# Gated outputs in both partition halves, a reordered opening, and a new list of attention steps, in a two-layer encoder step

## The chip, the core and the metric

One core of a Trainium2 chip runs the whole program in one launch. The metric is the device time of one execution in microseconds (us), lower is better. The core has a matrix engine (TensorE, PE in the rows; its weight loads are PEld), three engines for elementwise work (VectorE or DVE, ScalarE or ACT, GpSimd or POOL), a queue engine that issues transfers (SyncE or SP), the on-chip memory SBUF with 128 partitions, and PSUM, 128 partitions too, into which TensorE writes its products.

## What is computed

One step of a streaming encoder of two layers on 512 prompt tokens and 64 sample tokens (576 in all, width 1024, float32). Each layer:

```python
h = rmsnorm(x, g_mix_norm)
qa, ka, va, qg, kg, vg, ag, rg, cq, ckv, kr = split(h @ w_in)
o_a = rmsnorm(stick_breaking_attention(qa, ka, va))        # 4 heads x 64
o_b = rmsnorm(gla(qg, kg, vg, ag), g_gla_out) * silu(rg)   # gated linear attention, 4 heads, 32 -> 64
o_c = rmsnorm(mla(cq, ckv, kr))                            # latent attention, 8 heads x 64
x = x + concat([o_a, o_b, o_c]) @ w_out
x = x + cross_attention(rmsnorm(x), memory)                # 256 memory tokens
x = x + swiglu(rmsnorm(x))                                 # inner width 2816
```

Gated linear attention runs over blocks of 16 tokens. For a block with decayed queries `qt`, keys `kt`, and the state `S` (32 x 64 per head) that all earlier blocks left:

```python
att = where(tril, qt @ kt.T, 0)
o   = qt @ S + att @ v
S   = exp(b_last) * S + kd.T @ v
```

## The kernel before

All activations lie transposed, features on partitions and the 576 tokens along the row. The tokens are cut in two ways: five tiles (`TILES`: four of 128 tokens and one of 64), and two halves of `HF` = 288. Big products are made in about float32 from three products of rounded parts (`mm3`: high by high, high by low, low by high); the parts of an operand, H and L, are made by a copy on ScalarE and a subtraction on VectorE (`split_w`, `XNorm.split`). Small products are plain float32; each such call shows as two passes, two weight loads and two matmuls, in the trace.

**The opening.** SyncE loads three token tiles (`xin`), the first 256 columns of the input projection (`w_first`, buffer `wraw`, 1 MB), and the other two token tiles. TensorE turns each tile with eight transposes; the two evictions of a tile go to ScalarE and VectorE; ScalarE also sums the squares of each tile's rows (`x_squares`). `split_w` cuts the weights into two parts of 128 columns, each rounded and subtracted, and the first half of the tokens is split between these parts (`xn0.split`). Then `x_rstd` brings the norm factors of the rows to all partitions: a diagonal matrix for each tile on VectorE, multiplied by a matrix of equal numbers on TensorE. During the opening the order of ScalarE, VectorE and GpSimd is fixed as it is written (`nc.chain`), that of TensorE is not. The first products follow in `win`, four groups of 24 matmuls: half 0 of the tokens with two groups of 128 columns, then half 1.

**The list of steps.** Within a layer's mixers the units of work are generators that are advanced one step at a time; `STEPS` is a list, written out and used for both layers, of which unit goes next. A capital letter is a task (W the input projection and later output projections' steps, G gains, S and Z old keys, T short turns), a small letter a line of units with its number: a prepares the gated stage, l makes its block states, m scans them (VectorE), n writes its outputs (two steps each: scores, then products), o is the output norm; b is stick-breaking; later letters follow. One step of W is a group of 24 matmuls or a token tile of a projection.

**The gated stage.** `states` makes the sums of each block, `scans` turns them into the states, kept in `U` as 64 x 33 numbers per partition, so that the state of one block is read with a stride of 33 elements (the sample's with a stride of 5). `out` makes the scores of a tile for all four heads, masks them on VectorE (a predicated copy), and then accumulates in one PSUM buffer `po` (tag T, three buffers):

```python
for h in range(4):
    mm(po[0:64, h, 0:rn], vg[0:rn, t, h * 64:h * 64 + 64], at[0:rn, h, 0:rn], h == 0, False)
for n in range(nb):
    mm(po[0:64, :, 16 * n:16 * n + 16], S, qtx[:, :, r0 + 16 * n:r0 + 16 * n + 16], False, n == nb - 1)
```

Four copies, by turns on ScalarE and VectorE, move two heads to partitions 0 to 63 of `G` and two to 64 to 127. Stick-breaking's `tile_attention` already writes the outputs of two heads into the two halves of a PSUM buffer, head by head in turn.

## Time and profile before

| what | value |
|---|---|
| time, median of 3 runs | 1663.23 us (1661.26 to 1664.08) |
| the profiled execution, its own time | 1666.25 us |
| its span, first to last instruction | 1664.5 us |
| mean granted clock of TensorE | 0.994 |
| busy share: TensorE, VectorE, ScalarE, GpSimd | 98%, 73%, 54%, 9% |

The profile is of one execution. A row of the timeline gives start, length, engine, line, operation, output and inputs by their names in the program (`gla0` is the gated stage of layer 0, `sb1` stick-breaking of layer 1), shapes, a count where like rows were merged, and in brackets how long the engine had stood before it and on whose work. Nearly everything passes through one recording helper, so all rows have line 209; they are told apart by names. Matmul ends are modelled and overlap, so the distance between starts is the better price. The granted clock is given as a share of full speed: 1.00 is 2.4 GHz and 0.50 is 1.2 GHz.

### The profile page before, as it was taken

The numbers are of one execution on the slowest core, as the hardware profiler recorded it, in microseconds if no ns is written. First come the engines' busy times: TensorE is split into PE (matmuls) and PEld (weight loads), VectorE is DVE, ScalarE is ACT, GpSimd is POOL, SyncE is SP. The second block draws the span as 40 slices with busy tenths as digits, with TensorE's granted clock in tenths as the row PEclk, the third lists the DMA queues.
The fourth block names the chain that finished last, engine by engine and source line by source line (L and its number), as shares of the span: only waits on it lengthen the run. The fifth ranks groups of instructions, "written<-read, shape, count | busy, mean of one in ns | idle before, by whom it ended". The sixth has DMA issues, their size and how long they took to land.

```text
span 1664.5 us, 30858 instructions
## 1 busy us (share of the span) xinstructions
PE 1638.2 (98%) x12279; PEld 1532.3 (92%) x12279; DVE 1216.0 (73%) x2508; ACT 897.1 (54%) x1915; POOL 142.2 (9%) x257
## 2 busy tenths in 40 slices
PE   8999999999999999999999999999999999999998
PEld 7989788699999999999998889877999999999998
DVE  5747798876798767666667488987678877667663
ACT  6436778665754443344443457886667453344431
POOL 3112351000000000000010133300000000000000
PEclk9999999999999999999999999999999999999999
DMA  5322230022123232322223313201211232332321
GB/s 168 118 69 65 75 111 26 27 77 77 52 77 102 77 102 77 102 93 85 81 75 97 93 40 118 67 27 39 89 52 56 97 102 77 102 99 79 101 77 58
DMA packets 113647, 133.30 MB, mean 80 GB/s; under 512 B 10610, under 2 KB 95712, under 8 KB 113504
## 3 DMA queue, kind: packets, MB, share of 16 engines
q1 hardware_dynamic: 113120, 131.30, 25.0%
q8 instruction: 97, 1.59, 0.4%
q14 instruction: 46, 0.38, 0.1%
q0 software_dynamic: 352, 0.03, 0.0%
q10 hardware_dynamic: 32, 0.01, 0.0%
HBM read 123.64 MB, written 7.68 MB: 79 GB/s over the span
## 4 chain that ended last, share of the span: by engine, by line
PE 81%; DVE 7%; issue 4%; ACT 3%; DMA 2%; POOL 1%; ACTq 0%; POOLq 0%; DVEq 0%
PE ffn0.D L209 10%; PE ffn1.D L209 9%; PE ffn0.T L209 7%; PE ffn0.S L209 7%; PE ffn1.T L209 6%; PE ffn1.S L209 6%; PE win1.D L209 6%; PE win0.D L209 4%; PE wout1.D L209 3%; PE wout0.D L209 3%; PE cross1.D L209 2%; PE cross0.D L209 2%; PE cross0.T L209 1%; PE cross1.T L209 1%; PE mlap0.T L209 1%
## 5 line engine op out<-in xcount | busy, mean ns | idle before, releaser
L209 ACT ACTIVATE ffn1.wH<-ffn1.wraw 128x1024 fp32r<-128x1024 f32 x64 | 59.4, 927 | 116.9 <-PE ffn1.T L209 61.7
L209 ACT ACTIVATE ffn0.wH<-ffn0.wraw 128x1024 fp32r<-128x1024 f32 x64 | 59.3, 927 | 111.5 <-PE ffn0.T L209 60.4
L209 DVE TENSOR_TENSOR ffn1.sL<-ffn1.sum,ffn1.sH 128x1024 fp32r<-128x1024 f32 x40 | 48.9, 1222 | 40.0 <-ACT ffn1.sH L209 39.9
L209 DVE TENSOR_TENSOR ffn0.sL<-ffn0.sum,ffn0.sH 128x1024 fp32r<-128x1024 f32 x40 | 48.9, 1222 | 39.6 <-ACT ffn0.sH L209 39.5
L209 DVE TENSOR_TENSOR ffn1.wL<-ffn1.wraw,ffn1.wH 128x1024 fp32r<-128x1024 f32 x64 | 67.6, 1056 | 8.3 <-ACT ffn1.wH L209 7.6
L209 DVE TENSOR_TENSOR ffn0.wL<-ffn0.wraw,ffn0.wH 128x1024 fp32r<-128x1024 f32 x64 | 67.5, 1055 | 8.3 <-ACT ffn0.wH L209 7.6
L209 PE MATMUL ffn0.D<-ffn0.bT,ffn0.sH 128*128 128x288 f32 x320 | 65.3, 296 | 0.1
L209 PE MATMUL ffn1.D<-ffn1.bT,ffn1.sH 128*128 128x288 f32 x320 | 65.1, 295 | 0.1
L209 ACT ACTIVATE ffn1.sH<-ffn1.sum 128x1024 fp32r<-128x1024 f32 x40 | 42.2, 1055 | 21.4 <-PE ffn1.S L209 21.2
L209 ACT ACTIVATE ffn0.sH<-ffn0.sum 128x1024 fp32r<-128x1024 f32 x40 | 42.2, 1055 | 21.1 <-PE ffn0.S L209 21.0
L209 POOL TENSOR_TENSOR win1.s<-win1.vg,rS 128x32 f32<-128x32 f32 (+1 forms) x5 | 2.9, 590 | 581.3 <-DVE win1.vg L209 580.2
L209 PEld LDWEIGHTS ffn0.D<-ffn0.bT,ffn0.sH 128*128 128x128 f32 x320 | 51.6, 189 | 1.0 <-ACT ffn0.part L209 0.6
L209 PEld LDWEIGHTS ffn1.D<-ffn1.bT,ffn1.sH 128*128 128x128 f32 x320 | 51.6, 189 | 0.7 <-ACT ffn1.part L209 0.6
L209 PE MATMUL ffn1.D<-ffn1.bT,ffn1.sL 128*128 128x288 f32 x160 | 47.5, 297 | 0.0
L209 PE MATMUL ffn0.D<-ffn0.bT,ffn0.sL 128*128 128x288 f32 x160 | 47.5, 297 | 0.0
L209 PE MATMUL win1.D<-win1.wH,ffn0.hH 128*128 128x256 f32 (+1 forms) x160 | 47.2, 295 | 0.0
L209 PE MATMUL win0.D<-win0.wH,in.hH 128*128 128x256 f32 (+1 forms) x160 | 47.1, 295 | 0.0
L209 PE MATMUL win0.D<-win0.wL,in.hH 128*128 128x256 f32 (+1 forms) x160 | 46.1, 288 | 0.3 <-DVE win0.wL L209 0.3
L209 PE MATMUL win1.D<-win1.wL,ffn0.hH 128*128 128x256 f32 (+1 forms) x160 | 46.1, 288 | 0.3 <-DVE win1.wL L209 0.3
L209 PE MATMUL win0.D<-win0.wH,in.hL 128*128 128x256 f32 (+1 forms) x160 | 45.9, 287 | 0.0
L209 PE MATMUL win1.D<-win1.wH,ffn0.hL 128*128 128x256 f32 (+1 forms) x160 | 45.9, 287 | 0.0
L209 ACT ACTIVATE ffn0.part<-ffn0.D 128x288 f32<-128x288 f32 x60 | 24.5, 409 | 38.4 <-PE ffn0.D L209 38.4
(972 smaller groups left out, 6522.2 us busy)
## 6 DMA issues: line engine op xcount, KB each, us to landing
ffn0.wraw<-in_w_gate_dram SPq DMA_DIRECT2D x11, 1024.0 KB, 5.3
ffn0.wraw<-in_w_up_dram SPq DMA_DIRECT2D x11, 1024.0 KB, 5.3
ffn0.wraw<-in_w_down_dram SPq DMA_DIRECT2D x11, 1024.0 KB, 5.1
ffn1.wraw<-in_w_gate_dram SPq DMA_DIRECT2D x11, 1024.0 KB, 5.3
ffn1.wraw<-in_w_up_dram SPq DMA_DIRECT2D x11, 1024.0 KB, 5.4
ffn1.wraw<-in_w_down_dram SPq DMA_DIRECT2D x11, 1024.0 KB, 5.0
win1.wraw<-in_w_in_dram SPq DMA_DIRECT2D x7, 1024.0 KB, 5.4
win0.wraw<-in_w_in_dram SPq DMA_DIRECT2D x6, 1024.0 KB, 5.7
```

The costliest lines, as they stand in the source:

```text
L209: r = fn(*args, **kw)
```

## The change

Three parts. First, in `out`, odd blocks of 16 tokens are accumulated in partitions 64 to 127 of `po` and even ones in 0 to 63: attention by values becomes eight calls of half the columns, the states' calls alternate by block, and the eviction becomes eight copies of half the width. Second, the opening turns tiles 0 to 2, splits the weights (loaded in two halves of 128 columns; both low parts on VectorE), and goes to the first product; tiles 3 and 4 are turned between the first and second product, the squares of tile 2 come after that, and the norm rows of tiles 0 to 2 after the second product. TensorE's order is now fixed too, until the last of the four products. Third, `STEPS` is another order of the same steps.

```diff
@@ -39,14 +39,14 @@
 
 
 STEPS = """
-W0*3 G0 W0*4 T0 W0 T1 W0 T2 W0 T3 a0 W0 T4 a0 W0 a0 W0*3 S0*2 l0 W0 l0 S0 l0*2 l1 W0 l1*3 l2 S0 W0 l2 W0 l2*2 l3 S0 W0
-Z0*2 l3*3 l4 S0 Z0 W0 l4*3 Z0 W0 m0 Z0 T5 T6 W0 Z0 m0 W0 n0 n1 T7 T9 n0 n2 n1 n3 n2 n4 n3 n4 T8 o0 W0 o1 o0 o1 i0 j0
-W0*3 b0 j0 W0*2 b1 b0 j0 W0*3 b0 b2 W0 b1 j0 W0 b1 W0 b3 b2 j0 T10 W0 b2 b4 b3 T11 T12 b3 b5 W0 b4 W0 b4 b6 T13 k0 b5
-k0 b5 b7 Y0 p0 b6 k0 T14 b6 Y1 p1 b7 k0 b7 Y2 c0*2 d0 d1 k0 c1 Y3 k0 d2 c1 k0 d0 d3 d1 d4 d2 d5 k0*2 k1 d3 d6 k1 d4 d7
-k1*2 d5 d8 k1*2 d6 d9 e0 k1 d7 k1*2 d8 k1 e1 e2 k1*2 d9 e1 e3 k1 e2 e4 k1*2 f0 e3 f1 e4 k1*2 k2 f0 f1 e5 k2 f0 f2 f1
-f3 k2 e6 e7 f2 f3 e6 e7 f2 f4 f3 f5 e8 k2 e9 f4 f5 k2 e8 f4 f6 f5 e9 f7 f6 f7 f6 k2 f8 f7 e10 k2 e10 f9 f8*2 f10 f9
-k2*3 f10 f9 f11 f10 f12 g0*2 f11 k2 f12 f11 f13 g1 f12 g1 k2 g2 f13 k2 g2 f13 g3 k2*2 g3 k2*2 h1 h0 k3 h2 h1*2 k3*2
-h0*2 h3 h1 h2 h0*2 h2 k3 h2 h1 h3 h2 h3 k3 h3*2 k3*13
+W0*3 G0 W0*4 T0 W0 T1 W0 T2 W0 T3 a0 W0 T4 a0 W0 a0 W0*3 S0*2 l0 W0 l0 S0 W0 l0*2 l1 W0 l1 W0 l1*2 l2 S0 l2 W0 l2*2 l3
+S0 W0 Z0*3 l3*3 l4 S0 Z0 W0 l4*3 W0 m0 Z0 T5 T6 Z0 m0 W0 n1 n0 T7 n0 n2 n1 n3 n2 T9 n4 n3 n4 T8 o0 W0 o1 o0 W0 o1 i0
+j0 W0*2 b0 j0 W0*2 b1 b0 j0 W0*3 b0 b2 W0 b1 j0 W0 b1 b3 W0*2 b2 j0 T10 b2 b4 b3 T12 b3 b5 W0 b4 W0 b4 b6 b5 k0 T11
+T13 k0 b6 b5 b7 Y0 p0 k0 T14 b6 Y1 p1 b7 k0 b7 Y2 c0*2 d0 d1 k0 c1 Y3 k0 d2 d0 k0 d3 d1 d4 d2 d5 k0*2 k1 c1 d3 d6 k1
+d4 d7 k1*2 d5 d8 k1*2 d6 d9 e0 k1 d7 k1*2 d8 e1 e2 k1*3 d9 e1 e3 k1 e2 e4 k1*2 f0 e3 f1 e4 k1*2 k2 f0 f1 e5 k2 f0 f2
+f1 f3 k2 e6 e7 f2 f3 e6 e7 f2 f4 f3 f5 e8 k2 e9 f4 f5 k2 e8 f4 f6 f5 e9 f7 f6 f7 f6 k2 f8 f7 e10 k2 e10 f9 f8*2 f10 f9
+k2*2 f10 k2 f9 f10 f11 f12 g0*2 k2 f11 f12 f11 f13 k2 g1 f12 g1 g2 f13 k2 g2 k2 f13 g3 k2 g3 k2*2 h1 h0 k3 h2 h1*2
+k3*2 h0*2 h3 h1 h2 h0*2 h2 k3 h2 h1 h3 h2 h3 k3 h3*2 k3*13
 """
 
 
@@ -339,7 +339,11 @@
     w_first = None
     for t, (c0, n) in enumerate(TILES):
         if t == 3:
-            w_first = fetch_w(I["w_in"][0, :, 768:1024], KD, 256)
+            w_first = clock.tile(wp.tile([128, 2048], F32, tag="wraw", name=nm("wraw"), bufs=2), "wraw", 2)
+            w_first = w_first.rearrange("p (k n) -> p k n", n=256)
+            for c in (0, 128):
+                nc.sync.dma_start(w_first[:, :, c:c + 128],
+                                  I["w_in"][0, :, 768 + c:896 + c].rearrange("(k p) n -> p k n", p=128))
         raw = big(name="xin")[:, 0:D]
         nc.sync.dma_start(raw[0:n, :], I["x_prompt"][0, c0:c0 + n, :] if t < 4 else I["x_sample"][0])
         xraw.append(raw)
@@ -347,7 +351,7 @@
 
     ident = cst([128, 128], "ident")
     make_identity(tc.nc, ident)
-    nc.chain.update(act=None, dve=None, pool=None)
+    nc.chain.update(act=None, dve=None, pool=None, pe=None)
     grow = u("kp", "grow")[0:84, 0:128]
     nc.vector.memset(grow, 1.0)
     for r0, g in ((16, "g_cross_norm"), (32, "g_ffn_norm"), (48, "g_mem_norm")):
@@ -429,7 +433,7 @@
             H, L = (clock.tile(wp.tile([128, 1024], F32R, tag=tag, name=nm(tag), bufs=WB[tag]), tag, WB[tag])
                     [:, 0:nk * ncol].rearrange("p (k n) -> p k n", n=ncol) for tag in ("wH", "wL"))
             copyA(H, raw[:, ks, cs])
-            tt(L, raw[:, ks, cs], H, SUB, nc.gpsimd if between and i else None)
+            tt(L, raw[:, ks, cs], H, SUB)
             parts.append((H, L))
             if between and i == 0:
                 between()
@@ -717,23 +721,32 @@
     def x_squares(t, n):
         act(pt4("sq")[0:n, :], xraw[t][0:n, :], AF.Square, scale=D ** -0.5, accum_out=ss[0:n, t:t + 1])
 
-    def x_rstd(t0, t1):
-
-        d = ps_("T")
+    def x_diags(t0, t1):
+
         diags = u("u", "dg")
         for t in range(t0, t1):
             n = TILES[t][1]
-            dg = diags[0:n, (t - t0) * 128:(t - t0) * 128 + n]
-            nc.vector.tensor_scalar(dg, ident[0:n, 0:n], ss[0:n, t:t + 1], None, op0=MUL)
-            mm(d[:, (t - t0) * 128:(t - t0) * 128 + n], ones_x[0:n, :], dg)
+            nc.vector.tensor_scalar(diags[0:n, (t - t0) * 128:(t - t0) * 128 + n], ident[0:n, 0:n], ss[0:n, t:t + 1], None, op0=MUL)
+        return diags
+
+    def x_rows(t0, t1, diags):
+
+        d = ps_("T")
+        for t in range(t0, t1):
+            n = TILES[t][1]
+            c = slice((t - t0) * 128, (t - t0) * 128 + n)
+            mm(d[:, c], ones_x[0:n, :], diags[0:n, c])
         c0, c1 = TILES[t0][0], sum(TILES[t1 - 1])
         copyA(xn0.rows[:, c0:c1], d[:, 0:c1 - c0], scale=float(D))
 
-    for t, (c0, n) in enumerate(TILES):
-        if t < 3:
-            x_squares(t, n)
+    def x_splits(a, k0, k1):
+        for k in range(k0, k1):
+            xn0.split(k, slice(a * HF, (a + 1) * HF))
+
+    def x_turn(t):
+        c0, n = TILES[t]
         for i in range(0, KD, 4):
-            d = ps_("DTS"[(2 * t + i // 4) % 3])
+            d = ps_("DTS"[(2 * t + i // 4) % 3] if t < 3 else "T")
             for j in range(4):
                 tr(d[:, j * 128:j * 128 + n], xraw[t][0:n, (i + j) * 128:(i + j + 1) * 128])
             src = d.rearrange("p (i c) -> p i c", c=128)[:, :, 0:n]
@@ -741,22 +754,50 @@
                 nc.vector.tensor_copy(X[:, i:i + 4, c0:c0 + n], src)
             else:
                 copyA(X[:, i:i + 4, c0:c0 + n], src)
-        def splits(k0, k1):
-            for k in range(k0, k1):
-                xn0.split(k, slice((t // 2 - 1) * HF, t // 2 * HF))
-
-        if t == 2:
-            rstd_small(ss[:, 0:3], 1.0)
-            w_first = split_w(w_first, between=lambda: splits(0, 4))
-            splits(4, KD)
-        if t == 4:
-            x_rstd(0, 3)
-            splits(0, KD)
-    for t in (3, 4):
-        x_squares(t, TILES[t][1])
-    rstd_small(ss[:, 3:5], 1.0)
-    x_rstd(3, 5)
-    nc.chain.clear()
+
+    for t in range(3):
+        x_turn(t)
+        if t < 2:
+            x_squares(t, 128)
+    w_first = split_w(w_first, between=lambda: x_splits(0, 0, KD))
+
+    def first_products(G):
+
+        ds = []
+        for p in range(2):
+            ds.append(ps_("D")[:, 0:HF])
+            for k in range(KD):
+                mm3(ds[p], w_first[0](k, p * 128, p * 128 + 128), w_first[1](k, p * 128, p * 128 + 128),
+                    xn0.h(k)[:, 0:HF], xn0.l(k)[:, 0:HF], k == 0, k == KD - 1)
+            if not p:
+                for t in (3, 4):
+                    x_turn(t)
+                x_squares(2, 128)
+                rstd_small(ss[:, 0:3], 1.0)
+                x_splits(1, 0, 4)
+                dg = x_diags(0, 3)
+                x_splits(1, 4, KD)
+        x_rows(0, 3, dg)
+        for p in range(2):
+            tt(G[:, p, 0:HF], ds[p], xn0.rows[:, 0:HF], MUL)
+        for t in (3, 4):
+            x_squares(t, TILES[t][1])
+        rstd_small(ss[:, 3:5], 1.0)
+        dg = x_diags(3, 5)
+        yield "d"
+        yield "d"
+        for p in range(2):
+            ds[p] = ps_("D")[:, 0:HF]
+            for k in range(KD):
+                mm3(ds[p], w_first[0](k, p * 128, p * 128 + 128), w_first[1](k, p * 128, p * 128 + 128),
+                    xn0.h(k)[:, HF:T], xn0.l(k)[:, HF:T], k == 0, k == KD - 1)
+        x_rows(3, 5, dg)
+        for p in range(2):
+            tt(G[:, p, HF:T], ds[p], xn0.rows[:, HF:T], MUL)
+        yield "d"
+        yield "d"
+        nc.chain.clear()
+
 
     class Order:
 
@@ -1059,6 +1100,10 @@
             st["krn"] = turn["pool"].tile([128, 288], F32, tag="krn", name=nm("krn"), bufs=1).rearrange("p (t c) -> p t c", c=32)
             w = load_w(wi[:, 768:1024], KD, 256) if l else w_first
             for a in range(2):
+                if not l:
+                    if not a:
+                        yield from first_products(G)
+                    continue
                 for p in range(2):
                     yield from ws_steps(w, p * 128, KD, xn.h, xn.l,
                                         lambda a, cs, d: tt(G[:, p, cs], d, xn.R[:, cs], MUL), [a])
@@ -1403,14 +1448,20 @@
                                           ps[0:rn, :, 0:rn])
                 yield "T"
                 po = ps_("T").rearrange("p (h c) -> p h c", c=128)
+
+                at5, po5 = (x[:, :, 0:rn].rearrange("p h (n b c) -> p h n b c", b=2, c=16) for x in (at, po))
                 for h in range(4):
-                    mm(po[0:64, h, 0:rn], vg[0:rn, t, h * 64:h * 64 + 64], at[0:rn, h, 0:rn], h == 0, False)
+                    for b in range(2):
+                        mm(po5[64 * b:64 * b + 64, h, :, b, :], vg[0:rn, t, h * 64:h * 64 + 64], at5[0:rn, h, :, b, :], h == 0, False)
                 for n in range(nb):
                     S = st["U"][:, :, 8 * t + n] if t < 4 else Us[:, :, n]
-                    mm(po[0:64, :, 16 * n:16 * n + 16], S, qtx[:, :, r0 + 16 * n:r0 + 16 * n + 16], False, n == nb - 1)
-                for p in range(2):
-                    copyA(G[0:64, 1 - p, r0:r0 + rn], po[0:64, 2 * p, 0:rn])
-                    nc.vector.tensor_copy(G[64:128, 1 - p, r0:r0 + rn], po[0:64, 2 * p + 1, 0:rn])
+                    b = n % 2
+                    mm(po[64 * b:64 * b + 64, :, 16 * n:16 * n + 16], S, qtx[:, :, r0 + 16 * n:r0 + 16 * n + 16], False, n >= nb - 2)
+                for b in range(2):
+                    for hh, copy in enumerate((copyA, nc.vector.tensor_copy)):
+                        dst = G[64 * hh:64 * hh + 64, 0:2, r0:r0 + rn].rearrange("p a (n b c) -> p a n b c", b=2, c=16)
+                        for p in range(2):
+                            copy(dst[:, 1 - p, :, b, :], po5[64 * b:64 * b + 64, 2 * p + hh, :, b, :])
 
             phase[0] = f"gla{l}"
             od.line([(["vg"], states(t, r0, rn), None) for t, (r0, rn) in enumerate(TILES)], 1, name="states", tag="T")
```

## Rows read from the trace of the kernel before

**Rows 1.** The page, part 1: engine, busy us, share of the span, instructions.

```profile
PE 1638.2 (98%) x12279; PEld 1532.3 (92%) x12279; DVE 1216.0 (73%) x2508; ACT 897.1 (54%) x1915; POOL 142.2 (9%) x257
```

**Rows 2.** Table by stage: stretch, busy us of each engine, granted clock, DMA.

```profile
12.00:13.00 1.00, 0.71 (x6) 0.72 (x7) 1.00 (x2) 1.00 (x3) 0.89 (x1) 0.92 1.38 150
...
19.50:20.00 0.50, 0.50 (x5) 0.50 (x5) 0.41 (x3) 0.00 (x0) 0.00 (x0) 0.83 1.09 338
...
172.00:174.00 2.00, 1.14 (x4) 0.29 (x2) 2.00 (x3) 1.10 (x3) 1.79 (x4) 0.82 0.00 0
```

**Rows 3.** Timeline of the gated stage, layer 0: start us, length, instruction, count.

```profile
105.55 1.09 PE L209 MATMUL gla0.T<-gla0.u,win0.vg 128*64 128x128 f32 x8
...
106.48 1.98 PE L209 MATMUL gla0.T<-gla0.qtx,gla0.U 128*64 128x64 f32 x16
...
108.39 1.12 PE L209 MATMUL gla0.S<-gla0.qtx,win0.G 128*128 128x512 f32 x2
...
108.80 0.28 DVE L209 COPY win0.G<-gla0.T 64x128 f32<-64x128 f32 x1 [2.78 <-ACT win0.G L209]
...
109.44 1.09 PE L209 MATMUL gla0.T<-gla0.u,win0.vg 128*64 128x128 f32 x8
109.62 0.73 DVE L209 COPY_PREDICATED gla0.u<-trilm,gla0.S 128x512 f32<-128x512 uint32 x1 [0.54 <-PE gla0.S L209]
...
119.30 0.68 PE L209 MATMUL gla0.T<-gla0.u,win0.vg 64*64 64x64 f32 x8
...
119.90 1.12 PE L209 MATMUL gla0.T<-gla0.qtx,win0.vg 128*64 128x64 f32 x8
...
120.95 0.44 PE L209 MATMUL win0.T<-ident,win0.sbk 128*128 128x128 f32 x2
...
121.31 0.22 DVE L209 COPY win0.G<-gla0.T 64x64 f32<-64x64 f32 x1 [0.69 <-ACT win0.G L209]
```

**Rows 4.** Waits of TensorE, 920 to 950 us: total us, times, longest.

```profile
PE gla1.T L209 <- ACT gla1.u L209: 0.7, 1, 0.7
```

**Rows 5.** Instructions on gla0.T, weight loads: ns min/median/max, first and last start.

```profile
L209 PEld LDWEIGHTS gla0.T<-gla0.qtx,gla0.U x64: 191/213/216, 106.4 to 119.0; 128*64 128x64 f32 x64
...
L209 PEld LDWEIGHTS gla0.T<-gla0.u,win0.vg x40: 129/137/137, 105.6 to 119.7; 128*64 128x64 f32 x32, 64*64 64x64 f32 x8
```

**Rows 6.** Timeline of TensorE, stick-breaking of layer 1.

```profile
1003.32 1.09 PE L209 MATMUL sb1.T<-sb1.PT,win1.sbv 128*64 128x128 f32 x16
...
1021.70 0.95 PE L209 MATMUL sb1.T<-sb1.PT,win1.sbv 128*64 128x64 f32 x20
```

**Rows 7.** Timeline of the opening.

```profile
5.85 0.60 ACT L209 ACTIVATE X<-in.D 128x512 f32<-128x512 f32 x1
...
8.05 1.05 ACT L209 ACTIVATE in.sq<-in.xin 128x1024 f32<-128x1024 f32 x1
...
10.46 1.06 ACT L209 ACTIVATE in.wH<-in.wraw 128x1024 fp32r<-128x1024 f32 x1 [0.60 <-DMA in.wraw<-in_w_in_dram]
...
11.55 1.29 DVE L209 TENSOR_TENSOR in.wL<-in.wraw,in.wH 128x1024 fp32r<-128x1024 f32 x1 [0.92 <-ACT in.wH L209]
...
12.29 0.66 PE L209 MATMUL in.D<-ident,in.xin 128*128 128x128 f32 x4 [2.46 <-DMA in.xin<-in_x_prompt_dram]
...
13.88 0.50 PEld L209 LDWEIGHTS in.S<-ident,in.xin 64*128 64x128 f32 x4 [0.52 <-issue]
...
14.93 0.61 PE L209 MATMUL win0.D<-in.hH,in.wH 128*128 128x288 f32 x1
...
23.20 1.38 DVE L209 SCALAR_TENSOR_TENSOR in.hL<-X,gT,in.hH 128x288 fp32r<-128x288 f32 x3
...
29.60 0.85 PE L209 MATMUL in.T<-in.dg,ones_x 128*128 128x128 f32 x4 [0.46 <-DVE in.dg L209]
...
32.16 0.29 PE L209 MATMUL win0.D<-in.hH,in.wL 128*128 128x288 f32 x1
```

**Rows 8.** Timeline of VectorE, 78 to 106 us: the last scan.

```profile
96.98 0.81 DVE L209 TENSOR_TENSOR_SCAN win0.vg<-win0.vg 128x320 f32<-128x320 f32 x1
```

## The prediction

> **What bounds the kernel now.** The page's busy shares come first: TensorE is busy for 98% of the span [rows 1]. So a change pays by taking time out of TensorE's own stream, or by closing one of its few gaps. The next view is the table by stage, with the granted clock: TensorE idles for 2.46 us in the opening, until 12.29; its clock then falls to half and comes back at about 19.7 us; it falls again near 173 us, in the thin part of the stick-breaking stage [rows 2, 7]. A mean clock of 0.994 over 1664.5 us loses 10 us, so about 20 us run at half speed: three stretches of some 6.8 us, the third at the same place of layer 1. The change touches the first and shifts the others. The third view is the timeline of the stage that writes the gated outputs [rows 3], where TensorE runs without a gap in layer 0; the wait list of layer 1 shows one wait of 0.7 us behind it, on the squares of the output norm [rows 4].
>
> **Part 1, the gated outputs.** For one tile of 128 tokens TensorE runs 8 passes of attention by values (four heads, two passes a call; 105.55 to 106.48, 0.93 us, 0.116 a pass), 16 passes of state by query (106.48 to 108.39, 1.91 us, 0.119 a pass), and the scores of a later tile (108.39 to 109.44, 1.05 us) [rows 3]. All outputs lie in partitions 0 to 63. A pass of the states has only 64 columns and costs as much as one of 128: its weights, read with a stride of 33 elements, load in 213 ns, where packed values of the same size take 137 [rows 5]. After the change blocks alternate between the two halves: attention becomes 16 passes of 64 columns, the states stay 16 passes, each on the other half from its neighbour.
>
> What an alternating pass costs stands in stick-breaking's own products, whose heads alternate between the halves. There 16 passes of 128 columns last 1.09 us, just what 8 of them last on one half; less a tail of 0.16 (1.09 against 0.93 above) that is 0.058 a pass against 0.116. And 20 passes of 64 columns last 0.95, less a tail of 0.08 (the last tile's 0.68 against 0.60 to the next start) 0.044 a pass, against 0.075 for that last tile, which has 64 columns on one half (8 passes from 119.30 to 119.90) [rows 3, 6]. The ratios are 0.50 and 0.59. For the states I take the worse: 0.119 becomes 0.070.
>
> One tile: attention 0.93 becomes 16 x 0.044 = 0.70, saving 0.23; states 1.91 become 1.12, saving 0.79; together 1.02, four times a layer, 4.1 us. The last tile, of 64 tokens: attention 0.60 becomes 0.70, losing 0.10; its 8 passes of states, 1.05 (119.90 to 120.95), become 0.62, saving 0.43 [rows 3]. A layer: 4.4 us, **both layers 8.8 us**. No row alternates halves with strided weights, so the bounds: at least the states save nothing, which leaves 4 x 0.23 - 0.10 = 0.82 a layer, 1.6 in all; at most they come down to the 0.044 of packed weights, which saves 1.21 + 0.23 a tile and 0.60 on the last, 6.4 a layer, 12.7 in all. A loss in the passes is excluded by the alternating rows, unless alternation fails altogether (attention then at 0.075 a pass).
>
> The evictions grow from four copies a tile to eight, in pairs by engine. Today VectorE's copy waits for ScalarE's, so the four are one chain, with a masked copy of 0.73 on VectorE in it; a copy of half the width takes 0.22 instead of 0.28 [rows 3]. Eight of these, three changes of engine at 0.04 and the masked copy make 2.6 us a tile. TensorE's period per tile goes from 3.89 to 0.70 + 1.12 + 1.05 = 2.87. The chain fits below that, with three buffers in PSUM between, so I cost it at nothing; if the cover went, every 0.1 us of chain above 2.87 would cost some 0.9 us over both layers' 4.5 tiles.
>
> A rule of the Trainium skill speaks against this part: TensorE: Matmul & The Clock Gate, Part 3, "The mechanism", says that a weight load overlaps with matmuls in flight only where the row group differs, and both halves here share their rows. By it the states' loads would stay as they are, the sum at the lower bound; the stick-breaking rows contradict it for packed weights, and no row decides it for strided ones.
>
> **Part 2, the opening.** Removed from the front: the squares of tile 2, and the transposes of tiles 3 and 4 before the first products. TensorE resumes at 12.29, when tile 3's transfer lands behind the weights; the first product is at 14.93, the last at 32.16 [rows 7]. In the new order ScalarE alternates evictions (0.60) and squares (1.05, and 0.2 for the read of the sum): from the first eviction at 5.85 its steps end at 6.45, 7.70, 8.30, 9.55, 10.15. Then the weights' high part (1.06) ends at 11.2, VectorE's low part (1.29) at 12.5, the activations' first low part (1.38 / 3 = 0.46) at 12.95 [rows 7]. The weights come in two halves; the whole was there at 10.46, so the first half is not late at 10.15 as long as packets of half the size don't slow it. The first product can go at about 11.7, the second waits to 12.95: useful work resumes some 0.45 us after today's 12.29. Gone are 0.52 us of idle between tiles 3 and 4, and 0.46 before the last norm rows (at 29.60) [rows 7]. What comes: in TensorE's new fixed order the norm rows stand between the first two products and the second two, and wait for a chain that begins only when tiles 3 and 4 are evicted: squares of tile 2 on ScalarE, four splits and the diagonals on VectorE. Squares 1.25, the first split on both engines 0.9, three more of 0.46 and a first diagonal of about 0.2 are 3.8 us; 24 products at 0.13 (a row's 0.29 overlaps the next; 0.44 at half clock) cover 3.1 of it. I put 0.7 us of wait there, with the second half's products queued behind it.
>
> The clock: today it fell after the idle 2.46 us and came back 4.8 us after products began (14.93 to 19.7) [rows 2, 7]. If products begin at 12.95 and it follows as it did, it is back at 17.75, 2 us sooner, and half speed costs half: 1.0 us gained. Bounds: nothing, or all 3.4 us if it doesn't fall. The opening: -0.45 + 0.52 + 0.46 - 0.7 + 1.0, **about 0.8 us**, between a loss of 0.5 and a gain of 3.4.
>
> **Part 3, the list.** It has the same 317 steps, 39 of them of the input projection (W); only their places differ. A projection step now stands between the two second steps of the output norm and covers layer 1's wait of 0.7 us [rows 4]: gain 0.7. Where gated scores begin, tile 1's go before tile 0's, so tile 0's masked copy (0.73) has only one short turn (0.4, as the turn at 120.95) to hide behind [rows 3]: about 0.35 a layer, 0.7 lost. One projection step of some 3 us leaves the time between the scans of the states and their use; the scans end at 97.8 and the states are first multiplied at 106.48 [rows 3, 8], so this costs nothing. Near 173 us two projection steps are moved ahead together, and the thin stretch behind them is no denser than before: I expect the clock to fall there as now.
>
> **The sum.** 8.8 + 0.8 + 0.7 - 0.7 = 9.6 us. The profiled execution took 1666.25, so 1656.65 in such an execution; the median of the runs shown is 3.02 below it, hence 1653.6.
>
> **The rivals.** (a) The strided loads stay serial: part 1 gives 1.6, the total is 2.4, time 1660.8. For it: a state pass costs as much as one of twice its columns, so its load is the bound already. Against: with packed weights alternation took the loads down too. Chance 0.22. (b) The opening gives nothing, or a thin stretch keeps the half clock 4 us longer: 1654.4 to 1655.6. Chance 0.18. (c) Slower: the evictions become the bound of the gated stage. The copies are one chain, and now move runs of 16 elements. To make the kernel slower by 0.2% the chain must exceed today's period of 3.89 by (3.3 + 0.8) / 9 = 0.46, so a copy must take (4.35 - 0.73) / 8 = 0.45 us, twice the 0.22 seen; at 0.55 the period is 5.1, which loses 1.2 x 4.5 x 2 = 11 us against the gain of 0.8: time 1673. Chance 0.08. The Trainium skill warns of this case in TensorEngine Tiling (Array Packing), "PSUM Bottleneck": tiling quickens TensorE and not the emptying of PSUM. (d) The states come down to packed cost: 12.7 for 8.8, time 1649.7. Chance 0.12. The forecast itself has 0.40.
>
> **How the numbers follow.** The runs of before spread over 2.8 us, so 0.2%, 3.3 us, is about what a measurement can tell from no change. Faster by more (below 1659.9) are the forecast, (b), (d) and a third of (a): 0.77. The rest of (a) lies within it: 0.15. Slower, above 1666.6, is (c), 0.08. The range runs from 1648, below (d), to 1661, just above (a); it leaves out (c), and (d) together with a clock that stays high in the opening.
>
> **What would show it.** The gated stage, 15.4 us from the first attention pass (105.55) to the transposes behind it (120.95), should become about 11; a state pass should start 0.07 us after the last, or 0.119 if (a) holds; if TensorE waits there on a copy, it is (c). In the opening the first product should stand near 11.7 us, the last near 31.4, with a wait on the diagonals between the halves, and the clock back before 18 us. Layer 1's wait on the squares should be gone. The prediction fails if the half-clock stretches of the stick-breaking stages grow or vanish, 3.4 us each, which nothing here fixes.

## The result and the profile after

The changed kernel takes **1644.80 us** (median of 4 runs, 1643.65 to 1646.05) against 1663.32 for the kernel before beside it; ratio 0.9891, 95% interval 0.9874 to 0.9908. That is 18.5 us less, where 9.6 were forecast, and below the range. The profiled execution has a span of 1644.3 us, its own time 1646.05, and a mean clock of 0.998 (0.994 before). It is the slowest of the four; the clock of the others is 0.999 to 1.000.

TensorE's row of the page, to be held against [rows 1]: 18.7 us of its busy time are gone, VectorE and ScalarE are where they were.

```profile
PE 1619.5 (98%) x12359; PEld 1515.4 (92%) x12359; DVE 1217.6 (74%) x2529; ACT 897.8 (55%) x1935; POOL 138.5 (8%) x256
```

The timeline of the gated stage of layer 0, against [rows 3]: 16 passes of attention from 105.54 to 106.06, 16 of the states from there to 107.00.

```profile
102.56 1.88 PE L209 MATMUL gla0.S<-gla0.qtx,win0.G 128*128 128x512 f32 x4
...
105.54 0.69 PE L209 MATMUL gla0.T<-gla0.u,win0.vg 128*64 128x64 f32 x16
106.06 1.12 PE L209 MATMUL gla0.T<-gla0.qtx,gla0.U 128*64 128x64 f32 x16
107.00 0.64 PE L209 MATMUL gla0.T<-gla0.u,win0.vg 128*64 128x64 f32 x16
107.21 0.33 ACT L209 ACTIVATE win0.G<-gla0.T 64x64 f32<-64x64 f32 x2 [2.13 <-PE gla0.T L209]
...
107.57 0.35 DVE L209 COPY win0.G<-gla0.T 64x64 f32<-64x64 f32 x2 [1.11 <-ACT win0.G L209]
...
113.46 0.66 PE L209 MATMUL gla0.T<-gla0.u,win0.vg 64*64 64x32 f32 x16
114.04 0.68 PE L209 MATMUL gla0.T<-gla0.qtx,win0.vg 128*64 128x64 f32 x8
114.65 0.44 PE L209 MATMUL win0.T<-ident,win0.sbk 128*128 128x128 f32 x2
```

A state pass now costs 0.059 us on average (0.94 / 16; 0.119 before), an attention pass 0.033 (0.52 / 16). A call is two passes, and the calls alternate between the halves; in the start times of the single passes they stand in pairs, 0.007 us apart, one pair every 0.118, where before they started singly, 0.12 apart. Where a product of full width comes next, as behind 107.46, the 16 state passes take 1.05. From the first scores to the transposes behind the stage, 102.56 to 114.65, it is 12.1 us; before it was 17.6 (103.31 to 120.95), and layer 1 has the same two lengths. The row of the state weights' loads has hardly changed from [rows 5]:

```profile
L209 PEld LDWEIGHTS gla0.T<-gla0.qtx,gla0.U x64: 192/214/219, 106.0 to 113.2; 128*64 128x64 f32 x64
```

The opening, TensorE's timeline, against [rows 7]; the input projection behind it begins at 31.80, before at 32.30.

```profile
11.23 0.40 PE L209 MATMUL win0.D<-in.hH,in.wH 128*128 128x288 f32 x1 [1.92 <-ACT in.hH L209]
12.49 0.61 PE L209 MATMUL win0.D<-in.hL,in.wH 128*128 128x288 f32 x1 [0.87 <-DVE in.hL L209]
...
23.89 0.91 PE L209 MATMUL win0.T<-win0.dg,ones_x 128*128 128x128 f32 x6 [0.39 <-ACT in.hH L209]
...
30.91 0.30 PE L209 MATMUL win0.D<-in.hH,in.wL 128*128 128x288 f32 x1
```

The table by stage (columns as in [rows 2]; the granted clock stands third from the end). The opening of this execution still has its half clock, from about 11.8 to 18.6. The stick-breaking work that stood around 173 us now comes 7 to 10 us sooner: the second twelve passes of the third tile's products by values ran in before from 171.32 on, the last ten of them only behind a wait of 0.86 us, and run in one go at 164.55 in after (TensorE's timelines, first of before, then of after). TensorE is nearly full there, and the clock stays.

```profile
173.67 0.69 PE L209 MATMUL win0.T<-ident,win0.j 128*128 128x128 f32 x2 [0.86 <-DVE sb0.PT L209]
174.29 1.54 PE L209 MATMUL sb0.T<-sb0.PT,win0.sbv 128*64 128x128 f32 x10
```

```profile
164.55 0.88 PE L209 MATMUL sb0.T<-sb0.PT,win0.sbv 128*64 128x128 f32 x12
```

The rows of the table, of after:

```profile
10.00:12.00 2.00, 0.40 (x1) 0.19 (x1) 1.26 (x3) 2.00 (x5) 0.00 (x0) 0.95 1.10 371
...
16.00:18.00 2.00, 2.00 (x10) 2.00 (x10) 0.58 (x1) 0.00 (x0) 0.00 (x0) 0.50 1.06 322
18.00:20.00 2.00, 2.00 (x18) 1.82 (x17) 0.53 (x1) 0.74 (x2) 0.00 (x0) 0.84 1.29 258
...
162.00:164.00 2.00, 1.94 (x10) 1.13 (x10) 2.00 (x4) 1.65 (x5) 1.89 (x3) 1.00 0.00 0
164.00:166.00 2.00, 2.00 (x16) 0.93 (x14) 2.00 (x4) 1.14 (x4) 0.69 (x2) 1.00 0.00 0
```

Landmarks with the same steps behind them in both kernels tell where the profiled executions part (after minus before): projection after the opening -0.5; first stick-breaking scores of layer 0 (132.2 and 125.9) -6.3; end of that stage (203.2 and 192.3) -10.9; first cross-attention scores (388.4 and 377.8) -10.6; first stick-breaking scores of layer 1 (952.5 and 934.5) -18.0; end of that stage (1022.4 and 1000.9) -21.5; end of the spans -20.2. So the gated stages with what surrounds them bring 5.8 and 7.4, the stick-breaking stages 4.6 and 3.5, and 0.3 and 1.3 are lost behind them.

### The profile page after: what moved, and what is told of

Its sections match the earlier page's. It is cut to its first block, busy times and chain, and to the rows that moved or that the text cites. A ratio compares the mean times of both kernels' runs of the same rounds, so it can differ in the third digit from the quotient of the medians.

```text
span 1644.3 us, 31065 instructions
## 1 busy us (share of the span) xinstructions
PE 1619.5 (98%) x12359; PEld 1515.4 (92%) x12359; DVE 1217.6 (74%) x2529; ACT 897.8 (55%) x1935; POOL 138.5 (8%) x256
## 4 chain that ended last, share of the span: by engine, by line
PE 88%; DVE 6%; ACT 2%; issue 2%; DMA 1%; POOL 1%; SPq 0%; POOLq 0%; ACTq 0%; DVEq 0%
PE ffn0.D L209 10%; PE ffn1.D L209 9%; PE ffn0.T L209 7%; PE ffn0.S L209 7%; PE ffn1.T L209 7%; PE ffn1.S L209 7%; PE win1.D L209 6%; PE win0.D L209 6%; PE wout0.D L209 3%; PE wout1.D L209 3%; PE cross1.D L209 2%; PE cross0.D L209 2%; PE cross1.T L209 1%; PE cross0.T L209 1%; PE mlap1.T L209 1%
## 5 line engine op out<-in xcount | busy, mean ns | idle before, releaser
L209 ACT ACTIVATE ffn0.part<-ffn0.D 128x288 f32<-128x288 f32 x60 | 24.6, 409 | 38.7 <-PE ffn0.D L209 38.7
L209 ACT ACTIVATE ffn1.part<-ffn1.D 128x288 f32<-128x288 f32 x60 | 24.5, 409 | 38.7 <-PE ffn1.D L209 38.7
```

Of the source, the lines that this page charges most:

```text
L209: r = fn(*args, **kw)
```

## The experiments

Each run reports a mean clock; (1 - clock) x span is the time that half speed took from it, in steps of 1.6 us, averaged over the runs ("half speed"). What is left of the mean time is the "rest", the work. The row of before is that of the runs beside the four single parts; beside the other kernels it lost 5.5 to 7.6 us to half speed, and its rest was 1655.4 to 1656.0. The split is rough: the end of a span, where TensorE has no work left, can be at half clock too and then counts up to 1.0 us too much (2.1 us of it in the profile of list_only). Differences below 1 us between two rows of either column are not read as an effect.

| kernel | median us (runs) | ratio, 95% | half speed | rest |
|---|---|---|---|---|
| before | 1662.6 (19, mean) | 1 | 6.8 | 1655.8 |
| after | 1644.80 (4) | 0.9891 [0.9874, 0.9908] | 1.6 | 1643.2 |
| gated_only | 1649.17 (4) | 0.9922 [0.9902, 0.9941] | 4.9 | 1644.3 |
| opening_only | 1658.83 (10) | 0.9983 [0.9970, 0.9995] | 4.5 | 1655.2 |
| list_only | 1657.51 (10) | 0.9972 [0.9963, 0.9982] | 4.6 | 1653.3 |
| no_list | 1648.08 (4) | 0.9917 [0.9899, 0.9934] | 4.9 | 1643.5 |
| sb_new | 1659.26 (11) | 0.9984 [0.9975, 0.9993] | 3.8 | 1655.5 |
| sb_old | 1647.56 (5) | 0.9918 [0.9904, 0.9932] | 4.0 | 1644.3 |
| warm | 1644.19 (4) | 0.9893 [0.9880, 0.9907] | 0.4 | 1643.7 |
| packed_after | 1640.10 (4) | 0.9868 [0.9853, 0.9884] | 2.1 | 1638.2 |
| packed_before | 1653.17 (4) | 0.9936 [0.9921, 0.9951] | 5.4 | 1647.4 |
| grouped | 1649.62 (4) | 0.9918 [0.9903, 0.9933] | 2.9 | 1646.8 |
| evict2 | 1649.99 (4) | 0.9918 [0.9903, 0.9933] | 1.2 | 1648.5 |
| packed_warm | 1639.49 (4) | 0.9859 [0.9843, 0.9876] | 0.4 | 1639.5 |
| fill | 1665.72 (12) | 1.0026 [1.0014, 1.0039] | 8.5 | 1657.2 |
| fill_warm | 1659.92 (12) | 0.9999 [0.9988, 1.0010] | 2.6 | 1658.5 |

**The parts, one by one.** Three kernels take one hunk of the change each into the kernel before (`out`, the opening, `STEPS`), and a fourth takes the new list back out of the changed one.

gated_only: 

> The kernel before with part 1 alone (old opening, old list). The gated stage, from its first scores to the turns behind it, goes from 17.6 us to about 12.1 in each layer by the rows of the changed kernel, so both theories take 11 us off. Theory 'order' (the half clock in the two stick-breaking stages hangs on the list's order of steps): the half-clock stretches stay, 1652. Theory 'phase' (it hangs on when the thin stretch comes, and the gated stage's saving moved it): they go, about 1645.5.

opening_only: 

> The kernel before with part 2 alone. Both theories: the last of the first products ends 1.2 us sooner, as in the changed kernel, and about half of that is lost again before the next weights are split; 1662.5 to 1663. Theory 'phase' adds that a shift of 1 us might already remove a half-clock stretch, 1659.

list_only: 

> The kernel before with part 3 alone, the new list with the old gated stage and old opening. Theory 'order': both half-clock stretches go (6.8 us) and the waits there shrink by about 1 us a layer, 1655. Theory 'phase': the stage starts when it did, the stretches stay, 1662 to 1664.

no_list: 

> The changed kernel with the old list. Theory 'order': the half clock is back in both stick-breaking stages, 1644.8 + 6.8 + 2 = 1653. Theory 'phase': it stays away, about 1646.

By the column of the rest the gated outputs bring 11.5 us of work and the list 2.5 by itself; the opening's 0.6, and the list's 0.3 on top of the other two, are too small to tell from nothing. All three kernels with one part lose about 2 us less to half speed than before (1.9, 2.3 and 2.2), the changed kernel 5.2.

So neither theory came out: gated_only and list_only lie between the two times they were given, and so does no_list. Only opening_only lies where 'phase' put it, and its profile shows that the opening itself gained, beside a fall near 171 us that is shorter than before's:

```profile
12.00:14.00 2.00, 1.57 (x10) 1.57 (x11) 2.00 (x5) 2.00 (x5) 0.00 (x0) 0.95 1.20 138
14.00:16.00 2.00, 2.00 (x10) 2.00 (x10) 2.00 (x5) 1.04 (x2) 0.00 (x0) 0.50 0.49 47
16.00:18.00 2.00, 2.00 (x14) 1.98 (x13) 0.52 (x1) 0.15 (x1) 0.00 (x0) 0.70 1.09 338
```

Half clock lasts 3.4 us here, from 13.8 to 17.2. With the old opening and no idle products it lasts 6.8 us in all six profiles (before, gated_only, list_only, sb_new, packed_before, fill); with the new one 3.4 us in six of seven (opening_only, no_list, sb_old, packed_after, grouped, evict2), and 6.8 in that of after alone.

**The order of stick-breaking's steps.** `sb_new` puts the new order of 29 steps, those behind the second step of b1 up to T14, into the kernel before; `sb_old` puts the old one into the changed kernel.

```diff
-b1 W0 b3 b2 j0 T10 W0 b2 b4 b3 T11 T12 b3 b5 W0 b4 W0 b4 b6 T13 k0 b5 k0 b5 b7 Y0 p0 b6 k0 T14
+b1 b3 W0*2 b2 j0 T10 b2 b4 b3 T12 b3 b5 W0 b4 W0 b4 b6 b5 k0 T11 T13 k0 b6 b5 b7 Y0 p0 k0 T14
```

sb_old: 

> The changed kernel, with the 29 steps of the stick-breaking stage (from b3 to T14) back in the old order and all else of the list new. Theory 'order' (the old order's waits and turns between products let the clock fall in some executions): 1648, with a mean granted clock near 0.997, as the run without the new list had. Theory 'elsewhere' (other parts of the list matter): 1645, clock 0.999.

sb_new: 

> The kernel before with only those 29 steps in the new order. Theory 'order': the clock's loss falls from 6.8 us to the 4.6 of the list alone, and some tenths of waits go: 1659.5 to 1660. Theory 'elsewhere': as before, 1662.6.

Both came out as theory 'order' said, and both move the time the way that the clock does: the new order takes 2.6 us of half speed off the kernel before (3.8 for 6.4 beside it) and leaves its rest as it was, the old one puts 2.3 onto the changed kernel, and 1.1 onto its rest. The old order does not bring the fall each time. Counting the two stick-breaking stages of each profile, the old order has a fall in 8 of 16 (before, gated_only, opening_only, no_list, sb_old, packed_before, fill, fill_warm), the new one in none of 16 (after, list_only, sb_new, warm, packed_after, grouped, evict2, packed_warm). Behind the stage the new list is not free of falls: in grouped the clock fell at 1037, behind a wait of 1.6 us on X that comes with the new list (0.2 with the old one):

```profile
1037.00:1040.00 3.00, 3.00 (x14) 2.60 (x14) 3.00 (x13) 1.46 (x5) 1.75 (x4) 0.55 0.00 0
```

Two rows of the table by stage, first of gated_only (layer 1), then of sb_old (layer 0): TensorE is about as thin in both, and the clock falls behind the first alone.

```profile
974.00:977.00 3.00, 1.90 (x7) 0.69 (x6) 2.87 (x5) 2.14 (x5) 2.84 (x6) 1.00 0.00 0
977.00:980.00 3.00, 3.00 (x19) 2.60 (x18) 3.00 (x7) 1.27 (x4) 0.00 (x0) 0.51 0.01 3
```

```profile
163.00:166.00 3.00, 2.13 (x14) 0.97 (x14) 3.00 (x5) 1.61 (x4) 2.31 (x4) 1.00 0.00 0
166.00:169.00 3.00, 3.00 (x29) 2.83 (x26) 3.00 (x7) 2.01 (x5) 0.00 (x0) 1.00 0.01 3
```

**Idle products in the opening.**

```diff
+    idle = ps_("S")
+    for _ in range(12):
+        mm(idle[:, 0:128], ident, ident)
     w_first = split_w(w_first, between=lambda: x_splits(0, 0, KD))
```

warm: 

> The changed kernel with 12 products of the identity by itself, results unused, in TensorE's idle stretch before the first products (about 2.6 us at full clock). If the fall in the opening comes from that idle stretch, the clock stays at 1.00 and the first products run at 0.13 a pass: 1.5 to 3 us faster in the executions that fell before, 1643 in the median. If it comes anyway, nothing changes: 1645.

The timeline shows them in place of the idle 1.92 us, and in the table by stage the clock is full:

```profile
9.55 2.84 PE L209 MATMUL in.S<-ident 128*128 128x128 f32 x24
```

```profile
12.00:14.00 2.00, 1.93 (x15) 1.72 (x14) 2.00 (x6) 2.00 (x6) 0.00 (x0) 1.00 1.23 138
```

The profile of this kernel has no half-clock stretch before its last 0.7 us, where TensorE has no work left, yet its median is only 0.6 below that of after: after's own runs had already lost only 1.6 on average. The idle products keep the clock up; that they make the changed kernel faster is not shown.

**What sets a pass.** In `packed_after` and `packed_before` the weights of the states' products are read as 64 neighbouring numbers, so other numbers are multiplied. `grouped` keeps both halves and sorts the passes by half.

```diff
-                    S = st["U"][:, :, 8 * t + n] if t < 4 else Us[:, :, n]
+                    S = st["Uf"][:, 64 * (8 * t + n):64 * (8 * t + n) + 64] if t < 4 else Usf[:, 64 * n:64 * n + 64]
```

```diff
-                for h in range(4):
-                    for b in range(2):
+                for b in range(2):
+                    for h in range(4):
...
-                for n in range(nb):
+                for n in sorted(range(nb), key=lambda n: n % 2):
```

packed_after: 

> The changed kernel with the states' weights read from 64 neighbouring numbers instead of with a stride (so it multiplies other numbers than the states). Theory 'load' (a pass of the states is paid by its strided load): a pass goes from 0.059 to the 0.033 of the attention passes, 72 passes of a layer save 1.9 us, two layers 3.7: 1641. Theory 'product': the stride doesn't matter, 0.059 stays, 1645.

packed_before: 

> The kernel before with the weights of the states' products read as 64 neighbouring numbers instead of with a stride (other numbers are multiplied, the work is the same). Theory 'load': the strided load sets the pass, on one half too; a pass falls from 0.119 to the 0.075 of 64 columns with packed weights, 144 passes, 6.3 us: about 1657. Rival 'columns or issue': the pass stays at 0.119 and the time at 1663.

grouped: 

> The changed kernel, with the outputs still in both halves, but the passes sorted by half: all of half 0 first, then all of half 1, for attention and for the states. Theory 'neighbours': a pass is quick only if the one before it stands on the other half. Then attention goes back to the 0.075 us a pass of 64 columns on one half (16 x 0.075 = 1.2 for 0.52 a tile) and the states to 0.119 (1.91 for 0.94): 1.65 us a tile, some 0.9 on the last, 7.5 a layer, 15 in all, so about 1660. Rival 'halves': it is the narrower output or the second half as such, and the order doesn't matter: about 1645, states still at 0.059 a pass.

Timelines, first of packed_after, then of packed_before:

```profile
105.44 0.64 PE L209 MATMUL gla0.T<-gla0.qtx,gla0.U 128*64 128x64 f32 x16
105.90 0.64 PE L209 MATMUL gla0.T<-gla0.u,win0.vg 128*64 128x64 f32 x16
```

```profile
106.40 1.09 PE L209 MATMUL gla0.T<-gla0.qtx,gla0.U 128*64 128x64 f32 x16
107.43 1.12 PE L209 MATMUL gla0.S<-gla0.qtx,win0.G 128*128 128x512 f32 x2
```

With packed weights (137 to 138 ns a load) a state pass costs 0.064 on one half (1.03 / 16) and 0.029 on two (0.46 / 16). Two halves halve the pass in both layouts: 0.119 to 0.059 strided, 0.064 to 0.029 packed. With the stride it is the load that sets the pass, since only the load was changed here. With packed weights it is not: under the same load of 137 ns a pass of 128 columns took 0.116 in before, one of 64 columns takes 0.064. These averages hold a fixed share for the ends of a group; inside it packed passes on one half start every 0.058 us, on two halves in pairs every 0.058. packed_before saves 8.0 us of work (1647.4 for 1655.4 beside it), more than the 6.3 expected, since 64 packed columns on one half cost 0.064 and not 0.075.

grouped lies between its two theories, 3.6 us of work above after. Its timeline:

```profile
104.28 0.79 PE L209 MATMUL gla0.T<-gla0.u,win0.vg 128*64 128x64 f32 x13
104.86 0.33 PE L209 MATMUL gla0.T<-gla0.qtx,gla0.U 128*64 128x64 f32 x1
104.91 0.28 PE L209 MATMUL gla0.T<-gla0.u,win0.vg 128*64 128x64 f32 x2
...
105.14 1.04 PE L209 MATMUL gla0.T<-gla0.qtx,gla0.U 128*64 128x64 f32 x11
...
108.23 1.12 PE L209 MATMUL gla0.S<-gla0.qtx,win0.G 128*128 128x512 f32 x2
```

All 16 attention passes of a tile stand ahead of its states in the kernel's text, yet state passes start between the last attention passes: the halves don't wait for each other pass by pass. Two tiles take 3.95 us (104.28 to 108.23), with calls that alternate 2.97 (105.54 to 108.51 in after's trace). So it is not the neighbour alone that counts; but of the two orders tried, the one whose halves stand farther apart overlaps less.

**The cover of the copies.**

```diff
-                        for p in range(2):
+                        for p in (0, 0, 1, 1):
                             copy(dst[:, 1 - p, :, b, :], po5[64 * b:64 * b + 64, 2 * p + hh, :, b, :])
```

evict2: 

> The changed kernel with every one of the eight evicting copies of a gated tile made twice. Theory 'thin cover': the chain of copies is 0.35 us a pair, 1.45 a tile, beside 0.74 of masked copy on VectorE, against TensorE's 2.5 us a tile; doubled it is 2.9 + 0.74 = 3.6, so 1.1 us over TensorE's period, 4.5 tiles, two layers: up to 10 us, less what three buffers take up: 1649 to 1655, with TensorE waiting on the copies. Rival 'wide cover': the copies lie beside other steps and nothing is seen: 1645.

Twice the copies cost 5.3 us of work. TensorE's list of waits, 100 to 140 us, was empty in after; here it has

```profile
PE wout0.T L209 <- DVE wout0.mL L209: 1.5, 1, 1.5
PE gla0.T L209 <- ACT gla0.u L209: 0.6, 1, 0.6
```

From the first scores to stick-breaking's first, 23.3 us (102.6 to 125.9) became 24.6 (100.9 to 125.5), with projection products pulled forward into the stage; that is 2.6 us in two layers, and where the rest of the 5.3 falls is shown only in part, by the wait on wout0.mL. The cover is there for eight copies and not for sixteen.

**Both savings together.** `packed_warm` joins packed_after and warm.

packed_warm: 

> The changed kernel with packed state weights (other numbers are multiplied) and twelve idle products of the identity before the first products. If both act as they did alone (packed about 5 us of work; idle products take away the half clock of the opening, some 1 to 3 us of clock where it falls): 1638 to 1640. If the idle products only shift work: 1640, as packed alone.

It is the fastest run, 0.6 us below packed_after, which the intervals don't separate. As a kernel it would need the states laid out with 64 neighbouring numbers a block; what that layout costs in the scans was not tried.

**The wait ahead of the fall.**

```diff
+                    for _ in range(2 if (i, h) == (3, 3) else 1):
-                    mm(ps, oSB[h // 2][r, cs], sbk[r, h // 2, 0:128 * (i + 1)])
+                        mm(ps, oSB[h // 2][r, cs], sbk[r, h // 2, 0:128 * (i + 1)])
```

fill: 

> The kernel before, with its own list and order, where one score product of stick-breaking (the fourth head of the fourth tile, two passes of 512 columns, 1.06 us) is made twice in place, so that TensorE works through the 0.86 us wait that stands ahead of the fall of the clock near 173 and 993 us. Theory 'the wait brings the fall': the half clock leaves both stick-breaking stages; the mean clock of the runs goes from 0.996 to 0.998 and the time falls by some 3 us, less 0.2 to 1 us a layer for the product and what it delays: about 1660 to 1661. Rival 'the thin stretch as a whole': it falls there as often as before, and the time is 1662 to 1664.

fill_warm: 

> The same, and twelve idle products of the identity after tile 2 of the opening, in TensorE's wait of 2.46 us for tile 3. If half clock can be kept out of all three stretches, the mean clock is 0.999 to 1.0 and the kernel before takes about 1656 to 1658 without any of the change; then some 6 of the change's 18.5 us are clock. If not, 1660 or more.

fill missed its aim. The second product was ordered behind the wait, as its timeline shows, and the wait of 0.87 stayed:

```profile
173.25 0.44 PE L209 MATMUL win0.T<-ident,win0.j 128*128 128x128 f32 x2 [0.87 <-DVE sb0.PT L209]
173.61 1.48 PE L209 MATMUL sb0.T<-sb0.PT,win0.sbv 128*64 128x128 f32 x10
175.03 2.07 PE L209 MATMUL sb0.S<-win0.sbk,win0.qo 64*128 64x512 f32 x2
```

So it says nothing on that wait, and shows only what more work there costs at half clock (2.07 for 1.06). fill_warm carries the same misplaced product. Its half speed is down to 2.6, though three of its twelve runs are still at 0.995 or 0.996, and its profile has no fall before its last 1.7 us, though the same wait stands in it:

```profile
171.47 0.44 PE L209 MATMUL win0.T<-ident,win0.j 128*128 128x128 f32 x2 [0.86 <-DVE sb0.PT L209]
```

The wait by itself doesn't bring the fall, then; sb_old's profile has it in both layers too (0.9 us each), and no fall. The median of 1659.9 is above the 1656 to 1658 expected by about the cost of the doubled products. With some 2.1 us for these taken off its rest (2 x 1.06), the old kernel's work is 1656.4, close to its rest in the other runs: the half speed can account for the remainder of its time.

## Why the prediction was too small

**Part 1, the gated outputs: right in kind, undersized.** Forecast 8.8, measured 11.1 in the trace (2 x (17.64 - 12.09)) and 11.5 by gated_only. The mechanism held; two terms of the sum were mis-sized. The larger is "attention 0.93 becomes 16 x 0.044 = 0.70": a pass came to 0.033, and the attention of four tiles went from 3.66 to 2.02 us a layer, 1.64 saved for 0.92 (the fourth tile's runs into a score product, which is counted with its old 0.43). The other is "For the states I take the worse: 0.119 becomes 0.070": it became 0.059, or 0.066 where a product of full width follows, and the states of four tiles went from 7.56 to 4.09 us, 3.47 saved for 3.16. The last tile's attention, put at a loss of 0.10, came out even (0.58 for 0.60). Of the 1.1 us missed in a layer, 0.7 lie in attention, 0.3 in the states and 0.1 in the last tile.

Both prices came from 64-column rows whose totals were divided by their counts. In the row of 20 passes [rows 6] the passes start in pairs every 0.058 us, 0.029 a pass; its 0.044 holds a gap of 0.15 where the weights change from 128 rows to 64, and another at its start. The last tile's 0.075 on one half is likewise a pass every 0.058 and the ends of a group of eight. Pass for pass the ratio is the plain half, in these rows too.

The stage was to be about 11 us from the first attention pass; it is 9.1, of which some 0.7 is that the scores of tile 1 now stand ahead of that pass.

**Rival (a), strided loads stay serial: refuted.** A load still takes 214 ns and yet a pass 0.059: the loads of the two halves run side by side, starting in pairs 0.007 us apart. This is the point at which the Trainium skill spoke against the change (TensorE: Matmul & The Clock Gate, Part 3, "The mechanism"); the measurement decides against that rule here. Another page of the skill, TensorEngine Tiling (Array Packing), "Key Properties", says that different tiles can load weights and multiply in parallel, and the trace agrees (0.119 to 0.059 with the load unchanged). Rival (d) was right that packed weights are worth more still, but that the change itself would bring them to the packed price was wrong.

**Rival (c), the copies: not the bound.** A pair takes 0.33 to 0.37, and TensorE waits for none. evict2 shows that the cover costed at nothing is real and thin.

**Rival (b), less from the clock: the other way.** Half clock became shorter in the opening of most executions and rarer in the stick-breaking stages.

**Part 2, the opening: right in kind, undersized in the clock.** The first product came at 11.23 (11.7 forecast), the last at 30.91 (31.4), the wait between the halves at 0.39 (0.7). The forecast was 0.8, that is 0.2 lost in work and 1.0 gained by the clock. The profiled execution gives 0.5, but that the two agree is luck: this execution has the long stretch of half clock. The ten runs of opening_only are 2.9 us below before in the mean, 0.6 of work and 2.3 of half speed. The step that failed is "If products begin at 12.95 and it follows as it did, it is back at 17.75". The profile of after is back later, at 18.6, and the other six with the new opening sooner, at 15.3 to 17.2. With the old opening, half clock ended at 17.9 in gated_only and at 19.7 in before, behind falls at 11.1 and 12.8: its end followed the fall and not the first product.

**Part 3, the list: here the mechanism failed.** The step is "Near 173 us two projection steps are moved ahead together, and the thin stretch behind them is no denser than before: I expect the clock to fall there as now". The stretch is denser: TensorE is busy for 1.94 of 2 us where that work had 1.14 [rows 2], and the clock fell there in no profile with the new order. The two transposes that waited 0.86 for stick-breaking's copies come later now and wait 0.4, and another wait grew (TensorE's waits of after, 40 to 300 us):

```profile
PE wout0.D L209 <- DVE X L209: 1.6, 1, 1.6
...
PE win0.T L209 <- DVE sb0.PT L209: 0.4, 1, 0.4
```

The grown wait, 0.2 before, stands in list_only and sb_old as well and not in sb_new, so steps outside stick-breaking's 29 bring it. The wait of layer 1 on the squares is gone as forecast, but the 0.7 us charged for the masked copy never came: TensorE waits on nothing in the gated stage.

**The sum.** By the table, the mean fell by 17.8 us: 12.6 of work (mainly part 1) and 5.2 of half speed. The forecast had 8.6 of work and 1.0 of clock, so it missed 4.0 and 4.2. Of the work, 2.3 to 2.7 are part 1; of the clock, the runs give about 2.3 to the opening (opening_only) and 2.2 to 2.6 to the list (list_only, sb_new), where the forecast had 1.0 and nothing. The profiled execution of before, with all three stretches at full length, was also taken as typical: its 0.994 is the low end of the runs seen (0.994 to 0.999). The text named vanishing half-clock stretches as what would make it wrong, and gave them no chance in the range.

**What stays open.** Why the clock falls in one execution of the old order and not in the next, and which of the 29 moved steps keeps it up. Why half clock in the opening lasts 3.4 us in most executions of the new one and 6.8 in the profile of after. Why gated_only, with the old list and the old opening, loses 1.9 us less to half speed. And the list's 2.5 us of work by itself, of which only 0.3 is left beside the other parts.

## What to carry to other kernels

Where small matrix products write to half of the output partitions, alternate the halves call by call: here that halved the price of a pass, strided weight loads included. Price such a pass by the distance between starts inside a group, not by the group's total over its count: the ends of a group, and a change of the weights' shape inside it, are in the total. And count half-clock stretches over several executions: one profile shows one throw, before and after, and an order of steps that avoids them can be worth as much as an edit.

## What the runs showed of the hardware

- The two output halves act like two lanes, each with its own price: 0.119 a strided pass and 0.064 a packed one on a half, 0.059 and 0.029 when both work, with the passes of the two halves starting 0.007 us apart. In grouped, state passes start ahead of attention passes that stand earlier in the kernel's text.
- Loading weights of 128 x 64 with a stride of 33 elements takes 214 ns for 138. Of these 76 ns, 55 appear in a pass on one half and 30 in one on two: packing was worth 8.0 us of work in the kernel before and 5.0 in the changed one.
- Half clock (1.2 GHz) lasted 6.8 us in six of six profiled openings of the old kind and 3.4 in six of seven of the new, and was absent in the three profiles where twelve idle products filled the idle time ahead of it (warm, packed_warm, fill_warm). In the stick-breaking stages some falls lasted 6.8 us and some 3.4 (no_list, from about 976.2 to 979.6).
- A gap of 0.15 us stood between passes where the weights changed from 128 rows to 64 (before, stick-breaking of layer 1, 1022.16 to 1022.31), against 0.058 from pair to pair ahead of it.
